# A decoder layer with PEER retrieval on one core: the residual of the last 256 tokens as DMA and VectorE work instead of products, and the first convolution rows fetched by ScalarE

## The chip, the core and the metric

The kernel runs on one core of a Trainium2 chip. The metric is the device time of one execution in microseconds (us). The engines are written as in the profile: PE (TensorE matmul; PEld is its weight load), DVE (VectorE), ACT (ScalarE), POOL (GpSimd), SP (SyncE). DMA transfers are issued by SP, ACT or POOL, each with a queue of its own (q1, q10 and q0 in the profile), and carried out by 16 DMA engines.

## The reference, cut to what matters

One layer, 512 prompt tokens and 32 sample tokens (8 sequences of 4), 1024 wide:

```python
proj = x @ w_in + b_in                     # q, k, v, g, ca, cg, 512 columns each
o, r_new = retention(rope(q), rope(k), v, r0)
ret_out = silu(g) * head_norm(o)
u = ca * sigmoid(cg)                       # depthwise convolution of width 31 over time
conv_out = silu(layer_norm(conv31(u) + dw_bias))
x1 = layer_norm(ALPHA * x + concat(ret_out, conv_out) @ w_out, ln1)
...
# PEER: 8 heads, the best 16 of 128 x 128 experts each
ffn = sum over the 128 chosen experts of gate * gelu(u[idx] . x1) * v[idx]
y = layer_norm(ALPHA * x1 + ffn, ln2)
```

The change touches two places of this: how `ALPHA * x1` gets into the last line for the last 256 prompt tokens, and how `u` gets into the convolution.

## The kernel before

The program is one function, `tile_step`, whose instructions a scheduler then orders on each engine by its own estimate of times; `behind(a, b)` fixes that `a` stands behind `b` where the author wants it, `await_` adds a wait. So an edit in one place can change the interleaving elsewhere.

**The first part** (up to about 400 us) is the projections, retention, convolution and output projection. A first pass handles 128 prompt tokens and the 32 samples, whose x1 is ready early; VectorE begins to retrieve experts for these (`gather0`) while the later tokens go through the mixer. The depthwise convolution of the later tokens (`later_conv`) runs on PE: for each of four channel groups m, `glu` makes u (line 290), `store_u` writes it to a DRAM tile `u_dram[m]` by a DMA of ACT (line 322), `tap_rows` fetches it back in four DMAs of SP, 206 KB each, each shifted by one column (line 330, tile `blk`), and `conv_taps` multiplies the rows by tap matrices (line 345, 64 records for one m). Nothing but the wait for the fetches separates `conv_taps` of m = 0 from the retention products (line 523) ahead of it. SP meanwhile issues weight loads (line 152) in program order.

**Then the mixer.** `mix_mm` computes the output projection and adds the residual as products: `residual` multiplies a 128-column block of x1 (or x), held transposed, by `scaled`, ALPHA on the diagonal (line 579). `mix_b` normalises (lines 560 to 574: `bn_stats`, `bn_aggr`, the subtraction, the reciprocal root, the scaling) and gives x1. For the first NG2 = 160 tokens (32 samples and 128 prompt tokens) it writes x1 to the DRAM tile `x1_dram` (line 967), from which it is loaded later. For the last 256 it keeps only the transposed copy `x1T`.

**Then the experts, in two ways at once.** The tokens up to NG2 and the first 128 are handled by *gathers*: POOL fetches a chosen expert's row of u and v (8 KB for each of 128 tokens, line 741), DVE takes the dot product (747), ACT the GELU and the gate (759, 764), DVE accumulates (769). The last 256 tokens, of which nearly all experts are computed densely, use PE: `scores_of` multiplies every expert's u with x1T (line 1039; SP loads u in 0.5 MB pieces at line 1037), `first_keys` and `last_keys` build the gates for each expert by products of one-hot matrices A and B (B by DVE, line 1156; products at 1175; the gates are then copied or multiplied into Ga to Gd at 1188 to 1191), and `v_products` accumulates gate times v over 128 groups of experts in four PSUM banks `pB` (line 1234; v loaded at 1229). The gathers beside it are released by `marks`, the products of the v stages, so that POOL doesn't run ahead.

Before the v stages start, `residual` fills the four banks `pB` with ALPHA * x1 by 16 calls, and all later products accumulate on top (`start=False`). The banks therefore hold the whole sum in the end, and the last norm reads them: `layer_norm(t, 128, ln[0], ln[1], pB[b], True)`, with the outputs stored by SP (line 1341). `phases` orders the last products so that b = 0 is complete first, then half 0 and half 1 of b = 1. `finish` is the same for the gathered tokens: it adds ALPHA * x1 to the accumulator by DVE (line 776) and normalises.

Of the kernel before, what the change touches and what calls it, by code (L numbers as in the profile page):

```python
# [8 lines left out]
F32 = mybir.dt.float32  # L9
# [7 lines left out]
OP = mybir.AluOpType  # L17
# [3 lines left out]
D = 1024  # L21
# [4 lines left out]
CW, CK = 512, 31  # L26
PH, NK, TK = 8, 128, 16
PAST = 4096
ALPHA = 2.0 ** 0.25
EPS = 1e-5  # L30
NR = NT - 128
NG2 = NS + 128
# [71 lines left out]
def tile_step(ctx: ExitStack, tc: tile.TileContext, a, o):  # L104
    nc = tc.nc
    V, S, T, G = nc.vector, nc.scalar, nc.tensor, nc.gpsimd

    per = ctx.enter_context(tc.tile_pool(name="per", bufs=1))
    gp = ctx.enter_context(tc.tile_pool(name="gp", bufs=3))
# [6 lines left out]
    dr = ctx.enter_context(tc.tile_pool(name="dr", bufs=1, space=bass.MemoryType.DRAM))  # L116
# [6 lines left out]
    banks = [ps0]  # L123
    turn = [0]

    steps, u_dram, updates, placed = {}, {}, [], []

    def mmps():
        turn[0] += 1
# [49 lines left out]
    ln = []  # L179

    def shared():
        return per.tile([128, 2 * D], F32, name="ln")
# [13 lines left out]
    def behind(ins, other):  # L196
        tc.add_manual_dep(ins.ins, other.ins.name, mybir.DependencyInfo(
            mybir.DependencyClass.NoSync, mybir.DependencyReason.DATA), reason="order")
# [29 lines left out]
    def rsqrt(dst, var):  # L228

        G.tensor_scalar(dst, var, EPS, None, op0=OP.add)  # L230
        G.tensor_tensor(dst, dst, mhalf[:dst.shape[0]].to_broadcast(list(dst.shape)), op=OP.pow)
# [4 lines left out]
    u_p = fe.tile([128, 4, CK + NP], F32, name="u_p")  # L236
# [82 lines left out]
    def store_u(m, L, p0):  # L319

        u_dram[m] = dr.tile([128, L + CK], F32, name=f"u_dram{m}")
        nc.scalar.dma_start(u_dram[m], u_p[:, m, p0:p0 + L + CK])

    def tap_rows(m, L, place):

        w = L + CK - 3
        rows = place[:, 0:4 * w].rearrange("p (g t) -> p g t", g=4)
        by_group = u_dram[m].rearrange("(g c) t -> c g t", g=4)
        for j in range(4):
            nc.sync.dma_start(rows[j * 32:j * 32 + 32], by_group[:, :, j:j + w])  # L330
        return rows

    def tap_weights(m):
# [219 lines left out]
    def layer_norm(t, n, g, b, src=None, table=False):  # L553


        st = gw.tile([128, 2, 6], F32, name="lst", bufs=3)
        mv = gw.tile([128, 2], F32, name="lmv", bufs=3)
        halves = [slice(q * 512, (q + 1) * 512) for q in range(2)]
        for q, c in enumerate(halves):
            V.bn_stats(st[:n, q], src[q][:n] if src else t[:n, c])  # L560
        V.bn_aggr(mv[:n], st[:n])
        rs = gw.tile([128, 1], F32, name="lrs", bufs=3)
        if table:
            S.activation(rs[:n], mv[:n, 1:2], AF.Sqrt, bias=eps_c[:n])
        else:
            rsqrt(rs[:n], mv[:n, 1:2])
        cs = halves if src else [slice(0, D)]
        for q, c in enumerate(cs):
            V.scalar_tensor_tensor(t[:n, c], src[q][:n] if src else t[:n, c], mv[:n, 0:1], g[:n, c],
                                   op0=OP.subtract, op1=OP.mult)  # L570
        if table:
            V.reciprocal(rs[:n], rs[:n])
        for c in cs:
            steps["ln"] = V.scalar_tensor_tensor(t[:n, c], t[:n, c], rs[:n], b[:n, c], op0=OP.mult, op1=OP.add)

    def residual(bank, xT, blocks, c0):

        for j, k in enumerate(blocks):
            T.matmul(bank[:, j * 128:(j + 1) * 128], xT[:, k, c0:c0 + 128], scaled, start=(j == 0), stop=False,
                     skip_group_check=True)  # L580
# [133 lines left out]
            return sb  # L714
        return score_of

    gx2, fence, held, marks, dots, listed = [], [], {}, [], [], []
    turns = ({}, {})

    def hold(k, ins):  # L720
# [3 lines left out]
    def gather(x1, idx, gate, acc, slots):  # L724

        late = len(slots) == 128 and x1 is not x1_0
        for k in slots:
            if x1 is x1_0:
                pools = (gp, gp, gp, gx, per) if k < K5 else (gp, gp, gp, gx) if k < KX else (gp, gp, gp, per)
                if KX <= k < K4[0] or k >= K4[1]:  # L730
                    pools = (gp,)
            elif late:
                pools = (gp, gp, gp, per if k < FREE else gx2[0]) if k < 60 else (gp, gp, gp, gx2[0], bx)
            else:
                pools = (gp, gp, gp, per) if k < len(slots) - 4 else (gp,)
            pool = pools[k % len(pools)]
            t = shared() if pool is per else pool.tile([128, 2 * D], F32, name="g")
            at = step(k) if late and k >= FREE else -1
            while at >= len(marks):
                yield  # L740
            fetch = G.indirect_dma_start(out=t, out_offset=None, in_=a["uv"],  # L741
                                         in_offset=bass.IndirectOffsetOnAxis(ap=idx[:, k:k + 1], axis=0))
            if at >= 0:
                tc.add_manual_dep(fetch.ins, marks[at].ins.name, mybir.DependencyInfo(
                    mybir.DependencyClass.Sync, mybir.DependencyReason.DATA), reason="pace")
            act = gw.tile([128, 2], F32, name="act")
            dot = V.scalar_tensor_tensor(t[:, :D], t[:, :D], 1.0, x1, op0=OP.mult, op1=OP.mult, accum_out=act[:, 0:1])  # L747
            if x1 is x1_0:
                for k0, ins in held.items():
                    if k >= k0:  # L750
                        behind(dot, ins)
            elif at >= 0:
                behind(dot, fence[0])
            turn = int((k - TURNS[0]) // TURNS[1]) + 1 if late and k >= TURNS[0] else -1
            if late and turns[1]:
                behind(dot, turns[1][min(max(turn, 0), len(turns[1]) - 1)])
            dots.append(dot)
            wgt = gw.tile([128, 1], F32, name="wgt")
            gate_ = S.activation(act[:, 1:2], act[:, 0:1], AF.Gelu)  # L759
            if x1 is x1_0 and k >= GATED and "scores" in steps:  # L760
                behind(gate_, steps["scores"])
            if turn > 0:
                behind(gate_, turns[0][min(turn, len(turns[0]) - 1)])
            S.activation(wgt, act[:, 1:2], AF.Copy, scale=gate[:, k:k + 1])  # L764
            v = t[:, D:]
            if k == slots[0]:
                S.activation(acc, v, AF.Copy, scale=wgt)
            else:
                V.scalar_tensor_tensor(acc, v, wgt, acc, op0=OP.mult, op1=OP.add)  # L769
            yield  # L770
# [18 lines left out]
                        break  # L789

    x1_0 = per.tile([128, D], F32, name="x1_0")
    x1_dram = dr.tile([NG2, D], F32, name="x1_dram")
    E0 = per.tile([128, PH, TK], F32, name="E0")
    GT0 = per.tile([128, PH, TK], F32, name="GT0")
    I0 = per.tile([128, PH * TK], I32, name="I0")
# [21 lines left out]
    both = lambda d0, d: [(0, 128, d0), (128, 160, d)]  # L817
# [12 lines left out]
    w = W0[2]  # L830
# [17 lines left out]
    for q in range(2):  # L848
        c = slice(q * 512, (q + 1) * 512)
# [13 lines left out]
    x1T, xT = xT, xT[:, :, NS:]  # L863
    banks[:] = [ps0]
    led = []
    for h0 in range(0, PH, 2):
        w = load_w(a["w_query"], h0 * 256)
        qq = small("qe", [128, 4, 128], bufs=1)
        for hs in ([h0], [h0 + 1]) if h0 == 0 else ([h0, h0 + 1],):
            for h in hs:  # L870
                for s in range(2):
                    m = (h - h0) * 2 + s
# [4 lines left out]
            c = V.tensor_copy(I0[:, ss], E0.rearrange("p h k -> p (h k)")[:, ss])  # L877
# [49 lines left out]
    for k, i in SLOTS_BEHIND:  # L927
        for dot in dots[k:]:
            behind(dot, updates[i])
    behind(placed[4], updates[1])  # L930
    banks[:] = [ps]
    rope(load_win(0), 0, xT, n - NS, 160, [(0, n - NS, qT)])
    later_keys = rope_steps(load_win(1), 1, xT, n - NS, 160, [(0, n - NS, kT)])
# [24 lines left out]
    xrs, pms, room = {}, {}, keys_or_scratch()  # L958
# [4 lines left out]

    def mix_b(c0, m, after=None):
        mix_norm(xrs[c0], m, x1T, c0, pms[c0], after)
        if c0 < NG2:
            nc.sync.dma_start(x1_dram[c0:min(c0 + m, NG2)], xrs[c0][:min(m, NG2 - c0)])

    norm_rows("ln1")
    gate_heads(ons[1], gT, NS)  # L970
# [80 lines left out]
    for h0 in range(0, PH, 2):  # L1051
        qs[h0 // 2] = (qs0, qs1)[h0 // 2 % 2]
        if h0:
            w = load_w(a["w_query"], h0 * 256)
# [4 lines left out]
        p0 = h0 % 4 * NS  # L1059
# [171 lines left out]

    def v_products(e, vt, b, qs=(0, 1)):
        W = place(e)
        return [T.matmul(pB[b][q], W[:, b * 128:(b + 1) * 128], vt[:, q * 512:(q + 1) * 512], start=False,  # L1234
                         stop=(e == NK - 1), skip_group_check=True) for q in qs]

    def v_stage(e):
# [44 lines left out]
    def step(k):  # L1282

        return k * 19 // 16
# [43 lines left out]
    pdn[0] = ctx.enter_context(tc.tile_pool(name="pdn", bufs=2, space=PSUM, reuse_waits="tile"))  # L1328
    pacc = ctx.enter_context(tc.tile_pool(name="pacc", bufs=1, space=PSUM, reuse_waits="tile"))
    pB = [[pacc.tile([128, 512], F32, name=f"pB{b}{q}") for q in range(2)] for b in range(2)]  # L1330
    for b in range(2):
        for q in range(2):
            residual(pB[b][q], x1T, range(q * 4, q * 4 + 4), NG2 + b * 128)
    gx2.append(ctx.enter_context(tc.tile_pool(name="gx2", bufs=1, reuse_waits="tile")))
    run((phases(), 1), (fetched(), 1))
    for b in range(2):
        t = gp.tile([128, 2 * D], F32, name="g")[:, :D]
        layer_norm(t, 128, ln[0], ln[1], pB[b], True)
        for q in range(2):
            c = slice(q * 512, (q + 1) * 512)  # L1340
            nc.sync.dma_start(o[0][0, 256 + b * 128:384 + b * 128, c], t[:, c])


# [44 lines left out]
```

## Time and profile before

| what | value |
|---|---|
| runs | 1436.52, 1442.21, 1444.98 us |
| median | 1442.21 us |
| the profiled execution's own time | 1439.42 us |
| its span in the trace | 1437.6 us |
| mean granted clock of PE | 0.993 |
| DMA | 511.01 MB, mean 355 GB/s |

The span runs from the first to the last recorded event; the remaining 1.8 us of the execution's time lie around it. All rows below are of that one execution. In a row of the timeline stand the start in us, the busy time in us, the engine, the line, the operation, what it writes and reads, how many instructions are drawn together, and in brackets the idle time of the engine just before and what ended it. "SPq" and "ACTq" are the issuing of DMAs. A row of the waits names the engine and line that waited, what released it, the sum in us, how often, and the longest. A row of windows has the window, its length, then busy time and instructions of PE, PEld, DVE, ACT and POOL, the granted clock of PE as a fraction of full speed, the busy share of the DMA engines and GB/s. A row of a DMA queue has packets, MB and their share of the engines' time.

Two pictures of the whole span help to place what follows. PE's busy tenths in 40 slices of 36 us stand in the first row, the clock in the second, the DMA engines' in the third:

```
PE   8999799999899999999999999999999999999998
PEclk9999899999999999999999999999999999999999
DMA  9859999988898799698699989999999999999995
```

### The profile page before, as it was taken

What the parts mean: (1) busy time and instruction counts of PE and PEld (TensorE: products, weight loads), DVE (VectorE), ACT (ScalarE), POOL (GpSimd) and SP (SyncE); (2) the same over time, 40 slices, a digit from 0 to 9 for tenths busy, and PEclk for the clock granted to TensorE, in tenths of its full rate; (3) what the DMA queues carried; (4) which work ended last, traced back from release to release, by engine and by line L of the source; (5) the groups of instructions that cost most, each with busy time, mean ns of one, the idle gap of its engine ahead of it and who ended that gap; (6) DMA issues with size and microseconds to landing.
All of it is one profiled execution on the core that took longest, in us unless ns stands there. A gap on an engine that the chain in (4) does not pass through costs nothing.

```text
span 1437.6 us, 19703 instructions
## 1 busy us (share of the span) xinstructions
PE 1395.3 (97%) x6766; PEld 960.1 (67%) x6766; DVE 1160.8 (81%) x2796; ACT 464.3 (32%) x1392; POOL 416.6 (29%) x407
## 2 busy tenths in 40 slices
PE   8999799999899999999999999999999999999998
PEld 8887365578667588887788884434445666666443
DVE  5949968988669999989999996987886966666666
ACT  1424422372122232244455541224653211111111
POOL 2172324334432222323123222233222222222220
PEclk9999899999999999999999999999999999999999
DMA  9859999988898799998699989999999999999995
GB/s 350 318 206 380 309 277 405 408 308 292 318 375 335 270 367 384 377 414 333 216 401 369 360 334 342 411 417 358 397 371 373 389 418 405 413 408 396 415 402 197
DMA packets 103281, 511.01 MB, mean 355 GB/s; under 512 B 10599, under 2 KB 24167, under 8 KB 60293
## 3 DMA queue, kind: packets, MB, share of 16 engines
q0 software_dynamic: 43392, 309.32, 55.2%
q1 hardware_dynamic: 54461, 193.48, 35.5%
q10 hardware_dynamic: 5328, 6.96, 1.4%
q8 instruction: 53, 0.87, 0.2%
q14 instruction: 47, 0.39, 0.1%
HBM read 503.49 MB, written 6.65 MB: 355 GB/s over the span
## 4 chain that ended last, share of the span: by engine, by line
PE 48%; DVE 26%; DMA 14%; issue 7%; ACT 3%; POOL 2%; SPq 0%; DVEq 0%; ACTq 0%; POOLq 0%
PE pB L1234 18%; PE sp L1039 17%; PE mm L255 8%; DVE acc L769 7%; DVE g L747 5%; DMA g<-in_uv_dram,Ib 4%; DMA g<-in_uv_dram,I 4%; DVE g L316 2%; PE mm L1175 2%; POOL g L741 1%; DMA ln<-in_uv_dram,I 1%; DMA cst<-in_consts_dram 1%; DMA blk<-u_dram 1%; PE mm L594 1%; DVE iu L640 1%
## 5 line engine op out<-in xcount | busy, mean ns | idle before, releaser
L1039 PE MATMUL sp<-x1T,uv 128*128 128x256 f32 x2048 | 460.5, 381 | 5.6 <-ACT Gb L1190 5.0
L1039 PEld LDWEIGHTS sp<-x1T,uv 128*128 128x128 f32 x2048 | 383.9, 190 | 71.8 <-issue 11.2
L769 DVE SCALAR_TENSOR_TENSOR acc<-g,wgt,acc 128x1024 f32<-128x1024 f32 x252 | 322.4, 1279 | 62.6 <-ACT wgt L764 60.7
L747 DVE SCALAR_TENSOR_TENSOR g<-g,x 128x1024 f32<-128x1024 f32 x255 | 309.9, 1217 | 64.7 <-DMA g<-in_uv_dram,Ib 34.2
L741 POOL DMA_INDIRECT g<-in_uv_dram,Ib x126 | 140.2, 1113 | 394.5 <-PE pB L1234 147.0
L759 ACT ACTIVATE act<-act 128x1 f32<-128x1 f32 x288 | 58.0, 202 | 565.1 <-DVE g L747 514.4
L741 POOL DMA_INDIRECT g<-in_uv_dram,I x104 | 136.6, 1314 | 302.2 <-DVE acc L769 177.7
L1234 PE MATMUL pB<-uv,Ga 128*128 128x512 f32 x352 | 158.9, 595 | 0.0
L255 PE MATMUL mm<-x1T,w 128*128 128x384 f32 (+1 forms) x448 | 152.7, 498 | 0.0
L255 PEld LDWEIGHTS mm<-x1T,w 128*128 128x128 f32 x448 | 84.5, 190 | 63.2 <-issue 31.2
L1234 PE MATMUL pB<-uv,Gb 128*128 128x512 f32 x256 | 111.6, 595 | 0.7 <-DMA uv<-in_uv_dram 0.5
L1234 PEld LDWEIGHTS pB<-uv,Ga 128*128 128x128 f32 x352 | 65.7, 190 | 66.6 <-issue 64.6
L1234 PE MATMUL pB<-uv,Gd 128*128 128x512 f32 x256 | 110.0, 592 | 0.0
L1234 PEld LDWEIGHTS pB<-uv,Gb 128*128 128x128 f32 x256 | 48.0, 190 | 63.5 <-issue 56.0
L1234 PEld LDWEIGHTS pB<-uv,Gd 128*128 128x128 f32 x256 | 48.6, 190 | 60.8 <-issue 59.3
L1234 PE MATMUL pB<-uv,Gc 128*128 128x512 f32 x160 | 72.2, 600 | 0.2
L1140 ACT ACTIVATE A<-row,e1T 128x128 f16<-128x128 bf16 x216 | 65.8, 391 | 5.9 <-PE mm L1175 5.8
L1188 ACT ACTIVATE W<-sp 128x256 f32<-128x256 f32 (+25 forms) x84 | 26.7, 318 | 120.2 <-PE sp L1039 118.7
L255 PE MATMUL mm<-g,w 128*128 128x160 f32 (+1 forms) x512 | 65.3, 287 | 0.0
L255 PEld LDWEIGHTS mm<-g,w 128*128 128x128 f32 x512 | 64.4, 191 | 0.6
L741 POOL DMA_INDIRECT g<-in_uv_dram,Is x25 | 33.6, 1344 | 77.5 <-DVE acc L769 38.7
L1191 DVE TENSOR_TENSOR Gd<-Gd,W 128x256 f32<-128x256 f32 x32 | 13.6, 424 | 48.4 <-ACT W L1188 48.4
(326 smaller groups left out, 1707.5 us busy)
## 6 DMA issues: line engine op xcount, KB each, us to landing
uv<-in_ut_dram SPq DMA_DIRECT2D x128, 512.0 KB
uv<-in_uv_dram SPq DMA_DIRECT2D x128, 512.0 KB
w<-in_w_in_dram SPq DMA_DIRECT2D x18, 1024.0 KB
w<-in_w_query_dram SPq DMA_DIRECT2D x15, 1024.0 KB
w<-in_w_out_dram SPq DMA_DIRECT2D x7, 1024.0 KB
blk<-u_dram SPq DMA_DIRECT2D x16, 206.0 KB
ln<-in_ln_g_dram POOLq DMA_DIRECT2D x5, 512.0 KB
ln<-in_ln_b_dram POOLq DMA_DIRECT2D x5, 512.0 KB
```

The lines of the kernel that those rows point to most:

```text
L255: T.matmul(p[:, :n], w[m // 2][:, k, (m % 2) * 128:(m % 2 + 1) * 128], xT[:, k, c0:c0 + n], start=(k == 0), stop=(k == 7))
L316: V.scalar_tensor_tensor(y[:, m], u_p[:, m, p0 + k:p0 + k + L], dw[:, m, k:k + 1], y[:, m], op0=OP.mult, op1=OP.add)
L594: last = T.matmul(banks_[q][:, s * 256:(s + 1) * 256], src[:, k, c0:c0 + C], wo[q * 2 + s][:, k0 + k, :], start=(xT is None and k0 == 4 an ...
L741: fetch = G.indirect_dma_start(out=t, out_offset=None, in_=a["uv"], in_offset=bass.IndirectOffsetOnAxis(ap=idx[:, k:k + 1], axis=0))
L747: dot = V.scalar_tensor_tensor(t[:, :D], t[:, :D], 1.0, x1, op0=OP.mult, op1=OP.mult, accum_out=act[:, 0:1])
L759: gate_ = S.activation(act[:, 1:2], act[:, 0:1], AF.Gelu)
L769: V.scalar_tensor_tensor(acc, v, wgt, acc, op0=OP.mult, op1=OP.add)
L1039: mm = T.matmul(sp[:, i], u[:, k], x1T[:, k, NG2:], start=(k == 0), stop=(k == 7), skip_group_check=True)
L1140: made = S.activation(A[:, t], row, AF.Abs, bias=e1T[:, t1 + t:t1 + t + 1])
L1175: mm = T.matmul(pt[:, t % nt], A[t % TB], B[:, q, t % TB // 2, :, t % 2], start=(q == 0), stop=(q == 1))
L1188: S.activation(W[:, :n], sp[:, :n], AF.Gelu)
L1234: return [T.matmul(pB[b][q], W[:, b * 128:(b + 1) * 128], vt[:, q * 512:(q + 1) * 512], start=False, stop=(e == NK - 1), skip_group_check= ...
```

## The change

Three edits that belong to two ideas. First, `mix_b` stores all of x1 to a larger `x1_dram` (two more DMAs of 512 KB on SP), the four residual calls ahead of the v stages go, the first v product of each bank starts the sum, and behind the v stages ACT fetches the x1 of each half of the 256 tokens (two DMAs of 512 KB) into the upper half of the tile in which the norm works; DVE adds ALPHA times it to the bank, 512 columns at a time (four `scalar_tensor_tensor`), and the norm then reads the tile in SBUF instead of the banks. Second, the four fetches of rows m = 0 are issued by ACT instead of SP; the store of u for m = 1 is put behind the last fetch issued so far, and the gates of the gathers from the seventh on are put behind the fourth fetch, both without a wait.

```diff
@@ store_u, tap_rows
-        nc.scalar.dma_start(u_dram[m], u_p[:, m, p0:p0 + L + CK])
+        store = nc.scalar.dma_start(u_dram[m], u_p[:, m, p0:p0 + L + CK])
+        if m == 1:
+            behind(store, fetched_[-1])
...
-            nc.sync.dma_start(rows[j * 32:j * 32 + 32], by_group[:, :, j:j + w])
+            load = (nc.sync if m else nc.scalar).dma_start(rows[j * 32:j * 32 + 32], by_group[:, :, j:j + w])
+            fetched_.append(load)
@@ gather
             gate_ = S.activation(act[:, 1:2], act[:, 0:1], AF.Gelu)
+            gates.append(gate_)
@@ behind later_conv
+    for gate_ in gates[6:]:
+        behind(gate_, fetched_[3])
@@
-    x1_dram = dr.tile([NG2, D], F32, name="x1_dram")
+    x1_dram = dr.tile([NG2 + 256, D], F32, name="x1_dram")
@@ mix_b
-        if c0 < NG2:
-            nc.sync.dma_start(x1_dram[c0:min(c0 + m, NG2)], xrs[c0][:min(m, NG2 - c0)])
+        nc.sync.dma_start(x1_dram[c0:c0 + m], xrs[c0][:m])
@@ v_products
-        return [T.matmul(pB[b][q], W[:, b * 128:(b + 1) * 128], vt[:, q * 512:(q + 1) * 512], start=False,
+        return [T.matmul(pB[b][q], W[:, b * 128:(b + 1) * 128], vt[:, q * 512:(q + 1) * 512], start=(e == 0),
@@ the end
-    for b in range(2):
-        for q in range(2):
-            residual(pB[b][q], x1T, range(q * 4, q * 4 + 4), NG2 + b * 128)
...
     for b in range(2):
-        t = gp.tile([128, 2 * D], F32, name="g")[:, :D]
-        layer_norm(t, 128, ln[0], ln[1], pB[b], True)
-        for q in range(2):
-            c = slice(q * 512, (q + 1) * 512)
+        both = gp.tile([128, 2 * D], F32, name="g")
+        t, x1 = both[:, :D], both[:, D:]
+        nc.scalar.dma_start(x1, x1_dram[NG2 + b * 128:NG2 + b * 128 + 128])
+        halves = [slice(q * 512, (q + 1) * 512) for q in range(2)]
+        for q, c in enumerate(halves):
+            V.scalar_tensor_tensor(t[:, c], x1[:, c], ALPHA, pB[b][q], op0=OP.mult, op1=OP.add)
+        layer_norm(t, 128, ln[0], ln[1], [t[:, c] for c in halves], True)
+        for q, c in enumerate(halves):
             nc.sync.dma_start(o[0][0, 256 + b * 128:384 + b * 128, c], t[:, c])
```

The scheduler's orders move with it; the rows below are instructions in the order of one engine, and from 322 on the line numbers of the changed kernel are 2 to 5 higher. On ACT, where the second and third u are stored (line 322; line 285 is the sigmoid of the gated unit, 759 and 764 the gate of a gather, 703 the exponential of a softmax), before:

```order
L703 ACT_TABLE_LOAD
L703 ACTIVATE ex<-ex 128x32
L322 DMA u_dram_1852<-u_p 128x415
L759 ACT_TABLE_LOAD
L759 ACTIVATE act<-act 128x1
L764 ACTIVATE wgt<-act,GT_135 128x1
L285 ACT_TABLE_LOAD
L285 ACTIVATE sg<-mm,cols 128x384
L322 DMA u_dram_1883<-u_p 128x415
```

And the same place on ACT in the changed kernel:

```order
L706 ACT_TABLE_LOAD
L706 ACTIVATE ex<-ex 128x32
L332 DMA blk<-u_dram_1815 32x4x412 x4
L322 DMA u_dram_1852<-u_p 128x415
L285 ACT_TABLE_LOAD
L285 ACTIVATE sg<-mm,cols 128x384
L762 ACT_TABLE_LOAD
L762 ACTIVATE act<-act 128x1
L768 ACTIVATE wgt<-act,GT_135 128x1
L322 DMA u_dram_1883<-u_p 128x415
```

The four fetches of m = 0 stand ahead of the store of m = 1, and one gate now follows the sigmoid where it came before it. On SP the four are gone from behind the weight loads.

On PE, the last scores ahead of the v stages (line 1039), the residual products and the first v products (line 1234) before:

```order
L1039 MATMUL sp<-x1T,uv 128x256 x16
L579 MATMUL pB_6864<-scaled,x1T 128x128 x4
L579 MATMUL pB_6865<-scaled,x1T 128x128 x4
L579 MATMUL pB_6866<-scaled,x1T 128x128 x4
L1039 MATMUL sp<-x1T,uv 128x256 x8
L579 MATMUL pB_6867<-scaled,x1T 128x128 x4
L1234 MATMUL pB_6864<-uv,Gb 128x512
L1234 MATMUL pB_6865<-uv,Gb 128x512
```

And in the changed kernel:

```order
L1180 LDWEIGHTS A
L1180 MATMUL mm<-B,A 128x96
L1044 MATMUL sp<-x1T,uv 128x256 x24
L1239 MATMUL pB_6866<-uv,Gb 128x512
L1239 MATMUL pB_6867<-uv,Gb 128x512
```

The 16 calls of line 579 are gone and the 24 scores around them stand together. Ahead of the first key groups on PE (line 1087 transposes the retrieved lists, line 214 is the warming of the clock with products of ones), before:

```order
L1087 MATMUL mm<-cst_89,eg 128x128 x2
L1039 MATMUL sp<-x1T,uv 128x256 x16
L1087 MATMUL mm<-cst_89,e_4246 128x128
L1087 MATMUL mm<-cst_89,eg 128x128 x2
L1039 MATMUL sp<-x1T,uv 128x256 x40
L214 LDWEIGHTS iot
```

And in the changed kernel:

```order
L1092 MATMUL mm<-cst_89,eg 128x128 x2
L1044 MATMUL sp<-x1T,uv 128x256 x16
L1092 MATMUL mm<-cst_89,e_4248 128x128
L1092 MATMUL mm<-cst_89,eg 128x128 x2
L1044 MATMUL sp<-x1T,uv 128x256 x32
L214 LDWEIGHTS iot
```

32 scores in place of 40 stand ahead of the warming; the other eight follow behind it, and from there to the v stages the scores and the key groups (line 1175) interleave in other portions. Elsewhere, on SP the two new stores of x1 stand between the fourth query weight load and the first four loads of u (line 1037). On ACT the two fetches of x1 stand between the last gate of the gathers and the square root's table load. On DVE the end reads: sum and statistics of half 0 of b = 0, the same of half 1, the norm of b = 0 with the sum of b = 1's half 0 ahead of its last two operations, then statistics of that half, the sum and the statistics of b = 1's half 1, and its norm.

More of the change, by code (lines that the diff above doesn't have):

```diff
@@ L124, in tile_step @@
     turn = [0]
-    steps, u_dram, updates, placed = {}, {}, [], []
+    steps, u_dram, updates, placed, fetched_ = {}, {}, [], [], []
     def mmps():
@@ L715, in fresh @@
         return score_of
-    gx2, fence, held, marks, dots, listed = [], [], {}, [], [], []
+    gx2, fence, held, marks, dots, gates, listed = [], [], {}, [], [], [], []
     turns = ({}, {})
```

## The prediction, made before the changed kernel ran

> **What bounds the kernel now.** I read the first part of the page, then the grouped waits of TensorE (PE), then the stages by windows.
>
> ```profile
> PE 1395.3 (97%) x6766; PEld 960.1 (67%) x6766; DVE 1160.8 (81%) x2796; ACT 464.3 (32%) x1392; POOL 416.6 (29%) x407
> PE 48%; DVE 26%; DMA 14%; issue 7%; ACT 3%; POOL 2%; SPq 0%; DVEq 0%; ACTq 0%; POOLq 0%
> PE mm L345 <- DMA blk<-u_dram: 6.3, 1, 6.3
> PE sp L1039 <- ACT Gb L1190: 5.0, 3, 2.7
> PE mm L620 <- DVE xr L574: 2.6, 1, 2.6
> PE mm L1175 <- DVE B L1156: 2.2, 7, 0.5
> 500.00:600.00 100.00, 99.80 (x474) 85.65 (x474) 99.94 (x335) 31.17 (x84) 27.79 (x23) 1.00 0.98 375
> 860.00:1040.00 180.00, 178.00 (x648) 80.12 (x647) 147.04 (x366) 61.63 (x173) 53.45 (x45) 1.00 0.97 382
> ```
>
> PE is busy for 1395.3 of 1437.6 us, so it is the bound by the mean: 42.3 us of idleness in all, the longest single wait being the 6.3 us of the convolution's first products (L345) for their rows. But the chain of waits gives PE only 48%. In 500 to 600 PE works 99.80 us of 100 and VectorE (DVE) 99.94; in 860 to 1040 PE works 178.00 of 180 while the DMA engines are busy 0.97 of the time. So a microsecond taken from PE counts only if DVE and the gathers don't hold it back a little later. That is the question for both halves of this change.
>
> **First rows, fetched by ACT.**
>
> ```profile
> 149.10 0.33 SPq L152 DMA_DIRECT2D w<-in_w_in_dram  x1
> 149.48 3.35 SPq L330 DMA_DIRECT2D blk<-u_dram  x4
> 150.77 0.23 ACT L703 ACTIVATE ex<-ex 128x32 f32<-128x32 f32 x1
> 155.08 0.34 ACTq L322 DMA_DIRECT2D u_dram<-u_p  x1
> 165.36 1.55 PE L523 MATMUL mm<-on,ktok 32*128 32x256 f32 x4 [1.60 <-DVE states L525]
> 173.26 8.02 PE L345 MATMUL mm<-blk,taps 128*32 128x384 f32 x64 [6.35 <-DMA blk<-u_dram]
> 230.70 5.37 PE L345 MATMUL mm<-blk,taps 128*32 128x384 f32 x64
> 150.00:155.00 5.00, 5.00 (x17) 2.91 (x16) 5.00 (x22) 0.98 (x2) 1.99 (x3) 1.00 1.01 326
> 165.00:170.00 5.00, 1.55 (x4) 0.83 (x4) 5.00 (x12) 2.38 (x9) 0.26 (x1) 0.50 1.01 366
> 177.00:179.00 2.00, 2.00 (x20) 0.82 (x16) 0.76 (x2) 0.00 (x0) 1.47 (x1) 0.58 1.03 415
> q1 hardware_dynamic: 190, 1.06, 81.3%
> q0 software_dynamic: 70, 0.57, 84.8%
> q1 hardware_dynamic: 71, 0.13, 20.8%
> 191.91 0.62 DVE L290 SCALAR_TENSOR_TENSOR u_p<-mm,cols,sg 128x384 f32<-128x384 f32 x1 [6.57 <-PE mm L255]
> ```
>
> Before, SP (SyncE) issues a 1 MB weight load at 149.10 and right behind it the four fetches of m = 0, 206 KB each. They land so late that PE, done at 166.91 (165.36 + 1.55), starts L345 at 173.26. Its granted clock is 0.50 meanwhile and until about 178.7 (a window of 2 us with 0.58), so the 64 products take 8.02 us where the same 64 take 5.37 at 230.70. So 6.35 of waiting and 2.65 of slow clock, 9.0 us, are the most that the fetches could return.
>
> How much of it? The last two queue rows are those of 156 to 158: the gathers' queue q0 sent 70 packets and SP's q1 71. They go one for one, 70 in 2 us, on 16 engines 0.45 us per pair. Each fetch is 128 runs, all four 512, or 32 per engine: 32 x 0.45 = 14.4 us, whichever queue holds them, as long as the gathers go on. What the new place saves is the time behind the weight load. The first queue row is of 150 to 154: SP's queue moved 1.06 MB, the weight load and hardly a row. At the 326 GB/s of 150 to 155 the load alone takes 3.2 us, so the rows began between 152.3 (149.10 + 3.2) and 154. After, ACT issues the four behind ex (150.77 + 0.23 = 151.0; as SP needs 3.35 for four, each takes 0.8 or so, the last at about 154), and the first can move at 151. The lead is 1.3 to 3 us; I take 2.0: L345 at about 171.3. The slow clock may end earlier by as much, or by more; I take 1.0 out of the 2.65. Together **-3.0**, with 0 and -9.0 as ends. Nothing queues up behind the new issues: the next ACT instruction of before was the store at 155.08, after an idle stretch for DVE. That store and those of m = 2 and 3 now stand behind the rows on ACT's queue; rows m = 1 wait for the first of them, but are needed only by the second L345 group, 18 us later.
>
> Does it last? DVE's row at 191.91 waits 6.57 us for PE, so DVE starts that stretch when PE does, and the gain passes to both engines.
>
> The Trainium skill's page "DMA: Bandwidth & Descriptors" (section "Issuing engines are not separate DMA queues") speaks against this half: DMAs started by different engines run on the same 16 DMA engines and interleave, and a second issuing engine saves only the sequencer's issue time. By that rule the term is 0 in place of -3.0. The one-for-one packets agree with the interleaving; that the weight load is served ahead on the same queue isn't covered by it.
>
> **Residual products removed.**
>
> ```profile
> 851.65 2.84 PE L579 MATMUL pB<-scaled,x1T 128*128 128x128 f32 x24
> 854.33 3.62 PE L1039 MATMUL sp<-x1T,uv 128*128 128x256 f32 x16
> 857.78 1.05 PE L579 MATMUL pB<-scaled,x1T 128*128 128x128 f32 x8
> 858.67 21.62 PE L1234 MATMUL pB<-uv,Gb 128*128 128x512 f32 x50
> 872.25 7.35 DMA x<-x_dram
> 885.53 12.74 DMA g<-in_uv_dram,Ib
> 1014.45 0.73 PE L1175 MATMUL mm<-B,A 128*128 128x32 f16 x16 [0.48 <-DVE B L1156]
> 1034.57 0.64 PE L1175 MATMUL mm<-B,ss 128*128 128x32 f16 x16 [0.36 <-DVE B L1156]
> 1035.40 0.73 PE L1175 MATMUL mm<-B,A 128*128 128x32 f16 x16 [0.20 <-DVE B L1156]
> ```
>
> The 16 calls are 32 records. They occupy PE from 851.65 to 854.33 and from 857.78 to 858.67: 2.68 + 0.89 = 3.57 us, with no idleness beside them. So the products of group b (L1234) start 3.57 us sooner. But at 1014.45, 1034.57 and 1035.40 PE waits for DVE's B: it comes there just in time already. DVE's work up to there runs through the load of x1 (7.35) and gathers (12.74), in pieces of the chain in time order, at a DMA share of 0.97, and the residual products aren't in that chain. What PE gains at 858 is waited off there as far as DVE isn't earlier too. DVE can be earlier a little, since the gathers of this stage are released by marks on PE's products. Ends -3.57 and 0; I take **-1.5**, nearer to the waits.
>
> **The tail.**
>
> ```profile
> 1422.83 0.70 DVE L560 BATCH_NORM_STATS2 lst<-pB 128x6 f32<-128x512 f32 x1 [3.54 <-PE pB L1234]
> 1413.37 1.29 DVE L776 SCALAR_TENSOR_TENSOR g<-x,acc 128x512 f32<-128x512 f32 x2
> 1414.58 1.28 DVE L560 BATCH_NORM_STATS2 lst<-g 128x6 f32<-128x512 f32 x2
> 1424.77 5.74 PE L1234 MATMUL pB<-uv,Gd 128*128 128x512 f32 x13
> 1430.55 0.70 DVE L560 BATCH_NORM_STATS2 lst<-pB 128x6 f32<-128x512 f32 x1 [2.35 <-PE pB L1234]
> 1431.53 1.41 DVE L569 SCALAR_TENSOR_TENSOR g<-pB,lmv,ln 128x512 f32<-128x512 f32 x2
> ```
>
> PE ends at 1430.51; from there everything is in line. One half of the sum is added by DVE after that: one more operation, at 0.65 (half of L776) to 0.70 (half of L569's 1.41, which reads PSUM, as this does). What follows reads SBUF: statistics 0.64 in place of 0.70, L569 1.28 in place of 1.41. Sum 0.70 - 0.06 - 0.13 = **+0.5** (0.4 to 1.4, the latter if the half before is late as well). The three other additions lie in the waits of 3.54 and 2.35 us. The two fetches of x1 stand on ACT behind the last wgt (about 1412); with the 7.35 us of the like load they are there by 1420, before 1422.83.
>
> **Stores of x1.**
>
> ```profile
> 373.00 27.53 SPq L1037 DMA_DIRECT2D uv<-in_ut_dram  x4
> 391.03 1.41 DVE L574 SCALAR_TENSOR_TENSOR states<-states,lrs,ln 128x512 f32<-128x512 f32 x2 [0.46 <-POOL lrs L231]
> 428.62 0.60 PE L1039 MATMUL sp<-x1T,uv 128*128 128x256 f32 x2
> ```
>
> On SP the two stores stand ahead of the first four ut loads, and the second waits until DVE has written its x1 (392.44). The loads begin there instead of at 373.00, but are first used at 428.62; the last of the four was issued about 400 anyway. 36 us cover a 0.5 MB load. I put it at 0; if that cover is gone, the same 1 MB as the weight load, 3 us. The added 2 MB are 0.4% of 511.
>
> **Order.** The scheduler also interleaves PE, ACT and DVE anew from about 430 to 860: 32 products L1039 rather than 40 stand ahead of the 24 warming ones, and groups of L1175 are cut elsewhere. No work is added; I put it at 0, within 3 either way (half of the 7.2 below).
>
> **Sum.** -3.0 - 1.5 + 0.5 + 0 = -4.0 on the profiled execution's 1439.42 gives 1435.4. That execution lies 2.8 us below the median shown (1442.21) and inside the runs' 1436.52 to 1444.98; I forecast 1436 us.
>
> **Rivals.**
>
> *Both gains in full*: the rows land in time (-9.0), DVE's B comes as much earlier as PE does (-3.57), tail +0.5: 1427.4. For it: PE is 97% busy and the wait stands alone. Against it: 32 rounds of 0.45 us, at a start of 152, end at 166.4 only if nothing else interleaves, and the store of m = 1 and the weight load's rest do. With one gain full and the other half, 1431.
>
> *Nothing arrives*: the rows are as late as before, since ACT issues 1.5 us later than SP did (151.0 against 149.48) and shares the same engines, and the 3.57 us end in the wait at 1014 to 1036; +0.5 from the tail: 1439.9. This is also the case in which the fetches don't do what they should. For it: one packet each per round; against it: the weight load's 3 us go.
>
> *Slower*: PE runs short at the first key groups. There it waits already for ACT's Gb (5.0) and DVE's B (7 waits, 2.2), both set by DVE, which is full in 500 to 600. With 8 products L1039 fewer ahead (8 x 3.62 / 16 = 1.8 us), PE arrives 1.8 us earlier and waits as much longer; if the newly cut groups double the waits too, 7.2 + 1.8 + 0.5 = +9.5, 1448.9 without any gain. It decides only from DVE not coming earlier by as much as PE; it becomes slower than before once the added waits pass 4.5 us. Against it: the products moved are still to be done later and fill other waits.
>
> **How the numbers follow.** Forecast (1431 to 1440) 0.50, both gains in full or nearly 0.24, nothing 0.14, slower 0.12. 0.5% is 7.2 us, about what a measurement of this kernel can tell from no change: the forecast's 4 lies within it. Faster by over 0.5%: the full case and some of the forecast, 0.32; slower 0.10; within, 0.58. The range takes in the full case at its low end, 1427, and reaches toward the slower one to 1446.
>
> **What would show it.** In the changed profile: L345's first group at 171.3 rather than 173.3, its 64 products at 7.0; a start before 168 would prove the full case, 173 or later the empty one. L1234 follows the last L1039 at once; the sum of waits of L1175 on B at 1010 to 1036 grows from 1.0 to about 3 if the gain is eaten there. From PE's last product to the end 0.5 us more than before. If PE's waits on Gb and B pass 12 us in 640 to 860, the slower case holds. If DVE in 300 to 500 waits more for gathers than before, then the gain at 173 was lost to DMA.

## The result, and the profile after

| | before | changed |
|---|---|---|
| median of 7 runs each | 1439.81 us | 1449.09 us |
| lowest and highest | 1436.36, 1444.98 | 1448.12, 1454.18 |
| profiled execution's span | 1437.6 us | 1446.3 us |

The ratio is 1.0058, 95% interval 1.0034 to 1.0082: the change costs 0.58%, about 8 us. In a second series of 13 runs beside 29 of before it was 1.0052 (1.0033 to 1.0071). That is slower than the range that was forecast, and on the other side of no change.

The grouped waits of PE, changed kernel (engine, line and what it makes, what released it: sum in us, times, longest):

```profile
PE mm L348 <- DMA blk<-u_dram: 6.2, 1, 6.2
PE mm L1180 <- DVE B L1161: 5.4, 8, 3.3
PE sp L1044 <- ACT Gb L1195: 4.3, 5, 1.3
PE mm L655 <- DMA keys<-in_keysT_dram: 4.0, 1, 4.0
```

The first row is the wait that the new fetches were to shorten: 6.3 before, 6.2 now. The last row is new. Before, no product waited for `keys<-in_keysT_dram`, a 1 MB load of the sub-keys that ACT issues for the key scores of the expert lists (L655, 652 before). The prediction didn't name it. What became of it, in the timelines of SP, ACT and PE of the changed kernel:

```profile
371.19 0.33 SPq L972 DMA_DIRECT2D x_dram<-keys  x1
388.21 0.33 SPq L972 DMA_DIRECT2D x_dram<-states  x1
388.85 8.65 SPq L1042 DMA_DIRECT2D uv<-in_ut_dram  x4
382.07 0.29 ACT L768 ACTIVATE wgt<-act,GT 128x1 f32<-128x1 f32 x1
389.36 0.20 ACT L762 ACTIVATE act<-act 128x1 f32<-128x1 f32 x1 [7.00 <-DVE g L750]
389.60 0.29 ACT L768 ACTIVATE wgt<-act,GT 128x1 f32<-128x1 f32 x1
389.81 0.35 ACTq L636 DMA_DIRECT2D keys<-in_keysT_dram  x1
402.26 1.62 PE L655 MATMUL mm<-keys,qs 128*128 128x128 f32 x6 [4.00 <-DMA keys<-in_keysT_dram]
405.81 1.80 PE L655 MATMUL mm<-keys,qs 128*128 128x128 f32 x10 [1.92 <-ACT qs L1007]
407.54 24.51 PE L255 MATMUL mm<-x1T,w 128*128 128x416 f32 x64
```

And the same place before:

```profile
374.62 0.36 ACTq L633 DMA_DIRECT2D keys<-in_keysT_dram  x1
401.93 0.83 PE L652 MATMUL mm<-keys,qs 128*128 128x128 f32 x6
404.75 1.05 PE L652 MATMUL mm<-keys,qs 128*128 128x128 f32 x10 [1.98 <-ACT qs L1002]
405.73 22.61 PE L255 MATMUL mm<-x1T,w 128*128 128x416 f32 x64
```

The key load goes into a tile that lies over the one from which the first added store reads (`x_dram<-keys`). So it now also has to wait for that store, and the scheduler put it two gates of gathers further back in ACT's queue: 59 gates stand ahead of it, not 57. The first of these waits 8.45 us for DVE, and DVE 8.27 of them for the gather (its dot product starts at 380.57); the second waits 7.00 us for DVE, which normalises the last x1 in between (384.91 to 388.19). The load is issued at 389.81 instead of 374.62, 1 us behind the first of the four loads of u, which itself waited on SP for the second store (the other three follow at 395 to 397). It arrives in a stretch in which the DMA engines are full. The DMA queues of the changed kernel from 394 to 400 (packets, MB, share of the 16 engines):

```profile
q10 hardware_dynamic: 123, 1.00, 39.8%
q0 software_dynamic: 132, 1.00, 39.4%
q1 hardware_dynamic: 146, 0.52, 21.4%
```

and before, in the same 6 us:

```profile
q0 software_dynamic: 306, 2.17, 98.1%
```

Before, the gathers had these 6 us alone and got 2.17 MB; now the keys (q10) and the loads of u (q1) take 61% and the gathers get 1.00 MB. So PE waits 4.00 us for the keys, and DVE 11.20 us for a gather where it waited 5.88 (changed, then before):

```profile
402.41 1.23 DVE L750 SCALAR_TENSOR_TENSOR ln<-ln,x 128x1024 f32<-128x1024 f32 x1 [11.20 <-DMA ln<-in_uv_dram,I]
```

```profile
401.35 1.23 DVE L747 SCALAR_TENSOR_TENSOR ln<-ln,x 128x1024 f32<-128x1024 f32 x1 [5.88 <-DMA ln<-in_uv_dram,I]
```

Part of the longer wait is that DVE came earlier. Counted from the first product on the samples' x1 (369.98 and 372.02, from PE's timelines), this row starts 3.1 us later than before.

The idle stretch has a second price. Windows of the changed kernel (PE, PEld, DVE, ACT, POOL busy, PE's granted clock, DMA share, GB/s), then of before:

```profile
400.00:407.00 7.00, 2.82 (x14) 2.28 (x16) 4.59 (x7) 1.90 (x7) 0.00 (x0) 0.58 1.03 424
407.00:415.00 8.00, 8.00 (x22) 4.22 (x19) 5.77 (x7) 1.30 (x5) 5.64 (x4) 0.72 0.88 327
403.00:411.00 8.00, 6.08 (x20) 3.52 (x19) 7.78 (x12) 3.19 (x12) 2.93 (x2) 0.50 0.92 348
```

```profile
400.00:407.00 7.00, 5.02 (x39) 4.03 (x39) 5.66 (x8) 3.22 (x11) 0.66 (x1) 1.00 1.01 415
```

The clock falls to half (0.50 from 403 to 411), and the 64 weight products behind it take 24.51 us instead of 22.61. To compare runs, whose start differs, I measure one stage: from the first product on the samples' x1 (`mm<-cst,xr`, 372.02 before) to the first score (`sp`, 428.62 before). It took 56.6 us before and 62.4 in the changed kernel (369.98 to 432.34).

### The profile page after: what moved, and what is told of

The parts are those of the page before. It is cut to its first block, busy times and chain, and to the rows that moved or that the text cites. A ratio compares the mean times of both kernels' runs of the same rounds, so it can differ in the third digit from the quotient of the medians.

```text
span 1446.3 us, 19656 instructions
## 1 busy us (share of the span) xinstructions
PE 1399.4 (97%) x6734; PEld 959.8 (66%) x6734; DVE 1163.0 (80%) x2800; ACT 460.8 (32%) x1391; POOL 428.5 (30%) x407
## 4 chain that ended last, share of the span: by engine, by line
PE 32%; DVE 17%; DMA 13%; issue 4%; ACT 1%; POOL 0%; DVEq 0%; POOLq 0%
PE pB L1239 19%; PE sp L1044 12%; DVE acc L773 5%; DMA g<-in_uv_dram,Ib 3%; DVE g L750 3%; DMA uv<-in_ut_dram 3%; DMA g<-in_uv_dram,I 3%; DMA g<-in_uv_dram,Is 2%; DMA uv<-in_uv_dram 1%; PE mm L1180 1%; DVE B L1161 1%; DVE ln L750 1%; DMA ln<-in_uv_dram,I 1%; DVE iu L646 1%; DVE iu L643 1%
## 5 line engine op out<-in xcount | busy, mean ns | idle before, releaser
L744 POOL DMA_INDIRECT g<-in_uv_dram,Ib x126 | 144.5, 1147 | 392.8 <-PE pB L1239 129.9
L744 POOL DMA_INDIRECT g<-in_uv_dram,I x104 | 143.9, 1383 | 295.9 <-DVE acc L773 158.4
L1239 PEld LDWEIGHTS pB<-uv,Gb 128*128 128x128 f32 x256 | 48.2, 190 | 62.2 <-issue 54.9
L744 POOL DMA_INDIRECT ln<-in_uv_dram,I x24 | 33.5, 1398 | 70.9 <-DVE acc L773 57.3
```

## The experiments

Theory K (keys): the loss is the late load of the keys. Rivals: G, the key groups that the scheduler cut anew (640 to 860); E, the end of the kernel (DMA at its limit from 1230 on, a longer tail). All ratios are to the runs of before on the same chip, with their 95% interval. A microsecond of loss is worked out as the ratio times 1444, the median of before in these series.

**The stores alone.** In the kernel before:

```diff
-    x1_dram = dr.tile([NG2, D], F32, name="x1_dram")
+    x1_dram = dr.tile([NG2 + 256, D], F32, name="x1_dram")
-        if c0 < NG2:
-            nc.sync.dma_start(x1_dram[c0:min(c0 + m, NG2)], xrs[c0][:min(m, NG2 - c0)])
+        nc.sync.dma_start(x1_dram[c0:c0 + m], xrs[c0][:m])
```

> The kernel before, with the two added stores of x1 and nothing else of the change (the residual stays in products, SP fetches the rows; what is stored isn't read). Theory K (keys): the stores put the 1 MB load of the keys behind two more gates on ACT, to about 392 in place of 374.6, where it collides with the loads of u that SP issues behind the second store; the first key products then wait for it and run at half clock. K expects 5 to 10 us more than before, the wait of the key products on the load at 3 to 7 us, and the first scores at about 434 in place of 428.6. Rival G (key groups): the loss comes from the newly cut first key groups around 658 in the changed kernel; then the stores alone cost under 2 us. Rival E (end): the loss comes from DMA at its limit in 1230 to 1310 and the longer tail; under 2 us here too.

Measured: 1.0043 (1.0020 to 1.0066), 6 us slower. Key load issued at 390.4, a wait of 4.45 us for it, 24.25 us for the 64 products, the stage 62.7 us:

```profile
403.28 1.62 PE L652 MATMUL mm<-keys,qs 128*128 128x128 f32 x6 [4.45 <-DMA keys<-in_keysT_dram]
408.55 24.25 PE L255 MATMUL mm<-x1T,w 128*128 128x416 f32 x64
```

So most of the loss comes with two stores that nothing reads, and not from the end of the kernel (E), which is as before here. Contrary to what was expected, this run doesn't separate G: the stores alone bring the new cut of the key groups as well. From the warming products to the first v product PE's order in the trace (residual products aside) is that of the changed kernel, record by record. The runs below with the keys early have this cut too, and they decide.

**Each half of the change alone.** First the half with the sum on DVE (the changed kernel with SP fetching the rows, and without the two orders on ACT):

```diff
...
-            load = (nc.sync if m else nc.scalar).dma_start(rows[j * 32:j * 32 + 32], by_group[:, :, j:j + w])
+            load = nc.sync.dma_start(rows[j * 32:j * 32 + 32], by_group[:, :, j:j + w])
...
-    for gate_ in gates[6:]:
-        behind(gate_, fetched_[3])
```

> The first half of the change alone: stores, no residual products, the sum on DVE at the end; SP fetches the rows as before. K expects the stores' 5 to 10 less up to 3.6 for the products plus 1 for the tail: 3 to 8 us slower than before. G: also slower if its first key groups are cut as in the changed kernel. If the stores are harmless, 3 to 0 us faster.

Measured: 1.0030 (1.0011 to 1.0049), 4 us slower, with a wait of 4.24 us for the keys and a stage of 62.8 us. Then the other half, the kernel before with the rows fetched by ACT:

```diff
...
-            nc.sync.dma_start(rows[j * 32:j * 32 + 32], by_group[:, :, j:j + w])
+            load = (nc.sync if m else nc.scalar).dma_start(rows[j * 32:j * 32 + 32], by_group[:, :, j:j + w])
+            fetched_.append(load)
...
+    for gate_ in gates[6:]:
+        behind(gate_, fetched_[3])
```

> The second half of the change alone: ACT fetches the first rows; residual products and stores as before. The load of the keys stays where it was on ACT. K expects 1 to 3 us faster than before: the first rows' products start about 1 us earlier and end about 2 us earlier. G or E: the same or slower, if the later stages don't pass the gain on.

Measured: 1.0015 (0.9991 to 1.0039), no difference that can be told, and no gain. PE waited 6.49 us for the rows. The keys were on time (issued at 377.7, no wait for them). The stage still took 58.6 us and the 64 products 24.31, behind a wait of 2.57 us for ACT's copy of the queries: the slow clock comes without late keys as well.

**The keys moved ahead.** In the changed kernel:

```diff
+        load = steps["keys"] = q.dma_start(keys[0], a["keysT"])
...
             gates.append(gate_)
+            if x1 is x1_0 and k >= 57:
+                behind(gate_, steps["keys"])
```

> The changed kernel with one order added: the gates of the gathers from number 58 on stand behind the load of the keys on ACT. K expects the load issued at about 377 (when the store of the tile under it has landed) and landed before 390, no wait of the key products on it, and 5 to 8 us less than the changed kernel: 1441 to 1444. G and E expect the changed kernel's time, within 2 us.

Measured: 1.0015 (0.9994 to 1.0036) against the changed kernel's 1.0052 and 1.0058: some 5 to 6 us back by one order (the intervals just overlap). ACT's and PE's timelines of this run, at the place shown above:

```profile
381.39 0.35 ACTq L636 DMA_DIRECT2D keys<-in_keysT_dram  x1
401.88 0.49 PE L655 MATMUL mm<-keys,qs 128*128 128x128 f32 x2 [1.61 <-ACT qs L1009]
404.82 22.61 PE L255 MATMUL mm<-x1T,w 128*128 128x416 f32 x64
```

No wait on the keys, full clock, and the stage at 55.4 us. The load went at 381.39 and not at 377: ACT had nothing else to do from 375.5 on, and SP had issued the store of the tile under it at 373.53, 7.9 us earlier. So the load does wait for the store, and this alone costs nothing in the stage. SP's loads of u still stood behind the second store here (from 390.67), so in this stage their delay alone costs nothing.

**The changed kernel again**, beside the next runs:

> The changed kernel itself once more, beside the runs below on one chip. It should again be 5 to 12 us slower than before, with a wait of about 4 us of the key products on the load of the keys and their weight products at half clock (24 to 25 us for 64).

Measured: 1.0052 (1.0033 to 1.0071). Its profiled execution was the fastest of the 13, at a span of 1438.0, and still had a wait of 3.67 us for the keys, 24.27 us for the 64 products and a stage of 62.2 us. One execution's span says less than a stage does: between the two profiles of this same program lie 8 us, of which 3 to 4 fall between 640 and 860 and as much again where DMA is at its limit behind 1230.

**The late keys alone.** The kernel before with only the load's place changed:

```diff
+        load = steps["keys"] = q.dma_start(keys[0], a["keysT"])
...
+            if x1 is x1_0 and k == 58:
+                behind(steps["keys"], gate_)
```

> The kernel before with one order added and nothing of the change: the load of the keys on ACT stands behind gate number 59 of the gathers, as in the changed kernel. Theory K (the late key load is the cause) expects 3 to 7 us more than before: the load issued at about 392, a wait for it or at least half a clock at the key products. If 1 to 2 us or nothing, then the load is harmless where SP's loads of u don't collide with it, and the collision behind the store counts.

Measured: 1.0011 (0.9987 to 1.0036), too little to tell. The load went at 387.08 with the loads of u already out (from 369.16). The stage was 60.5 us:

```profile
399.93 0.49 PE L652 MATMUL mm<-keys,qs 128*128 128x128 f32 x2 [4.06 <-ACT qs L1004]
404.38 23.99 PE L255 MATMUL mm<-x1T,w 128*128 128x416 f32 x64
```

PE waited for ACT's copy of the queries, which stood behind a gate whose gather was late; the keys' last packet had run by 397. So the stage is 3.9 us longer than before, by another way; with the loads of u behind the store it is 6. That the late load delayed this gather isn't shown. Over the runs with SP's or ACT's rows behind the weight load, the stage was 55.4 with u late and keys early, 60.5 with keys late and u early, 62.2 to 62.8 with both late (four profiles), and 55.9 to 58.6 with neither late (five, the three below with the keys ahead among them).

**Keys ahead, and the last store behind them on ACT**, in the changed kernel (the order of the run above, and):

```diff
-        nc.sync.dma_start(x1_dram[c0:c0 + m], xrs[c0][:m])
+        steps["kept"] = (nc.sync if c0 < known else nc.scalar).dma_start(x1_dram[c0:c0 + m], xrs[c0][:m])
...
     load_keys(pool=rk)
+    behind(steps["kept"], steps["keys"])
```

> The changed kernel with the load of the keys ahead of gate number 58, and the store of the last 128 rows of x1 issued by ACT behind it, so that SP's first loads of u don't wait for it. K expects no wait on the keys and the loads of u issued from about 371; the time 5 to 9 us below the changed kernel, within 3 of before. If the rest of the loss lies in the newly cut key groups at 640 to 860 (theory G), it stays 2 to 4 us above before.

Measured: 1.0021 (1.0005 to 1.0038), below the changed kernel, but 3 us above before. The stage is 55.9 us.

**The stores with both orders, without the rest**: the first experiment with the two orders of the last.

> The kernel before with the two added stores of x1 (not read), the load of the keys ahead of gate number 58, and the last store issued by ACT behind it. Theory K (the stores cost because they push the key load into the loads of u) expects what the stores alone cost, 0.43%, to go: within 2 us of before, and from the samples' x1 products (mm<-cst,xr) to the first scores 55 to 57 us, as before (56.6) and not 62.7. If the stores cost by themselves (1 MB more, DVE's x1 held longer), 4 to 6 us above before.

Measured: 0.9999 (0.9979 to 1.0018). Of the stores' 0.43% nothing is left that can be told. The stage is 57.2 us. The key groups are cut as in the changed kernel here too, so their cut isn't what the 0.43% came from.

**The same with the sum on DVE**, so that the way of adding the residual is the only difference from the last run:

> The same with the residual products removed and the sum on DVE at the end, the rows fetched by SP: the first half of the change without the late keys. From the stage itself: 3.6 us of products gone, 1.0 more in the tail, about 2 waited off on DVE's B at 1000 to 1040: 0 to 2 us below the run with the stores alone and the keys ahead. If all 3.6 count, 2.5 below; if the products are waited off entirely, 1 above.

Measured: 1.0009 (0.9994 to 1.0024): within 2 us of the last run and of before. The removed products bring nothing that the total shows. Against the same half with the keys late (1.0030) it is 3 us less, and the two intervals overlap; the stage is 58.2 us in place of 62.8.

**Rows ahead of the weights.** Two versions of the kernel before. In the first the loads of one weight block go behind the rows on SP (three loads moved), in the second only the load at 149.10:

```diff
-        w = load_win(2)
+        w = load_w(a["w_in"], 1024, after=steps["rows"][3])
```

```diff
-    rope(load_win(0), 0, xT, n - NS, 160, [(0, n - NS, qT)])
+    rope(load_w(a["w_in"], 0, after=steps["rows"][3]), 0, xT, n - NS, 160, [(0, n - NS, qT)])
```

> The kernel before with SP's weight loads of the block for v ordered behind the first rows' fetches, so that nothing stands ahead of the rows on SP's queue. If the 1 MB ahead held the rows back, their first packets leave within 1 us of the issue at about 149, and the first products start near 168 to 170. If each such fetch takes about 3.8 us from its issue to its first packet wherever it is issued, the packets begin at about 153 as before and the products start at 171 to 173. The weights come later, so the total may be longer.

> The kernel before with the first rows' fetches ahead of the one weight load on SP's queue (it follows them); nothing else. If a large load ahead holds back whatever queue follows it, the rows' first packets leave at about 150.5 in place of 153, and the first tap products start at 168 to 170 in place of 171 to 173: 2 to 5 us faster than before where the gain lasts. If the rows are held by the gathers' packets alone, no change.

Measured: the first 1449.44 us in its one run, the second 0.9994 (0.9978 to 1.0010). In both PE no longer waits for the first rows (in the first version it then waits 3.74 us for the second). In the second the products start right behind the retention products; but look at what is late next, in its PE timeline:

```profile
168.31 7.42 PE L345 MATMUL mm<-blk,taps 128*32 128x384 f32 x64
232.87 7.57 PE L345 MATMUL mm<-blk,taps 128*32 128x384 f32 x64 [4.84 <-DVE g L747]
```

There the last group's products (230.70 before, with no wait) wait 4.84 us for DVE's work beside the gathers, and run 7.57 us in place of 5.37. The samples' x1 then comes at 380.16, against 372.02. The 5 us of lead are gone, and the total is that of before.

**All three mended**: the sum on DVE, the keys ahead with the store behind, and the rows ahead of one load.

> All three mended: the sum on DVE, the keys ahead and the last store behind them, and the rows ahead of the weight load on SP. If the parts add up, faster than before by 2 to 6 us and faster than the changed kernel by 9 to 14. If DVE and the gathers set the middle stage (450 to 620), the early gains are given back there and it comes out within 2 us of before.

Measured: 1.0020 (0.9998 to 1.0042). The first rows' products start at 166.53, and the last group's at 231.08 with no wait: the lead is lost here as well, but before that place. No version beat the kernel before.

## Why the prediction was wrong, step by step

**The step that failed is the stores of x1**, put at 0. It followed the loads of u that wait on SP, found 36 us of cover for them, and that part held (stage 55.4 us with u late and keys early). It did not ask who else uses the tiles that the stores read. The key load does: it was on ACT's queue, its tile lies over one of them, and the new dependence moved it two gates back, into a full stretch of DMA. Price some 6 us: measured with the stores alone, and gone when two orders undo it, 1.0043 to 0.9999. The other pairs give 5 to 6 us (the changed kernel and the run with one order), 5 (with both orders) and 3 (the half with the sum on DVE), each to within about 4. So K is shown as the main cause. How the stage's 6 us reach the end isn't: the run with ACT's fetches alone and the second rows-first run come to the first score at 433.3 and 432.1, as late as the four with late keys (431.2 to 433.7), with no loss in the total that can be told. The fallback price of 3 us given there for a lost cover was for the wrong load.

**First rows, -3.0 taken, 0 measured.** The rows' wait was 6.35, 5.09, 4.16, 5.11, 4.29 and 3.40 us in the six profiles with SP's fetches behind the weight load, 4.7 on the mean, and 6.16, 6.49, 4.29, 3.03 and 5.83 in the five with ACT's, 5.2. On SP's queue the weight load ahead held the rows, as the working said: with the rows ahead of it the wait goes. What was wrong is that a queue of its own escapes it. The changed kernel's ACT timeline, then its DMA queues from 151 to 154 and from 154 to 156:

```profile
150.52 3.03 ACTq L332 DMA_DIRECT2D blk<-u_dram  x4
```

```profile
q1 hardware_dynamic: 106, 0.78, 70.2%
q0 software_dynamic: 23, 0.14, 21.8%
...
q0 software_dynamic: 70, 0.57, 73.6%
q1 hardware_dynamic: 19, 0.12, 15.1%
q10 hardware_dynamic: 46, 0.08, 10.2%
```

Issued at 150.52, the fetches have no packet until 154, when the weight load on q1 is nearly through; then they run one for one with the gathers, as forecast. By the packets of the traces, the rows' first one runs 5.4 to 5.9 us behind the issue of the weight load in the five profiles with ACT's fetches, and 3.9 to 4.0 in the six with SP's: ACT's rows begin later, not earlier.

The Trainium skill says in "DMA: Bandwidth & Descriptors" (section "Issuing engines are not separate DMA queues") that a second issuing engine saves only the time of issuing. The trace agrees in that nothing was gained: by that rule the term was 0. I had given the rival that carries it 0.14.

**And a gain there would not have lasted.** "DVE starts that stretch when PE does, and the gain passes to both engines" isn't borne out: with the wait removed, the lead is gone by 232.87, behind a wait of 4.84 us for DVE, and the total is unchanged (0.9994).

**Residual products: the size was close, the mechanism shown in part.** From the first v product to the first on Gd the seven profiles with the residual products take 460.5 us on the mean (459.4 to 461.8), the seven without 462.5 (460.1 to 464.3). So of the 3.57 us about 2.1 are given back behind 858, and some 1.5 stay, as forecast; the ranges overlap, so these means are good to little better than 1 us. Of the 2.1, 1.1 us lie between the first v product and the first on Ga, the stretch that holds the waits on B (192.2 against 191.1 us on the mean), and 1.0 between Ga and Gd (270.4 against 269.4). PE's waits on B from 1000 to 1045 us sum to 1.1 us on the mean without the products (0 to 2.4) and 0.7 with them (0 to 1.5), so B shows as a taker of some 0.4 only, and single profiles scatter by more than that. In the changed kernel they sum to 0.95, and not to the 3 that was named as the sign. That time is given back there agrees with the forecast; that B is what takes it was not shown, so the close size is in part luck.

**The tail: +0.5 taken, +1.0 measured.** From PE's end to the end of the span it is 7.0 to 7.2 us in the seven profiles with the residual products and 8.05 to 8.11 in the seven without. DVE of the changed kernel:

```profile
1438.23 0.69 DVE L1344 SCALAR_TENSOR_TENSOR g<-g,pB 128x512 f32<-128x512 f32 x1 [0.71 <-PE pB L1239]
1438.95 0.69 DVE L563 BATCH_NORM_STATS2 lst<-g 128x6 f32<-128x512 f32 x1
1439.92 1.41 DVE L572 SCALAR_TENSOR_TENSOR g<-g,lmv,ln 128x512 f32<-128x512 f32 x2
```

The addition is 0.69, as taken. The savings weren't there: the statistics take 0.69 and the subtraction 1.41 out of SBUF, as out of PSUM. The 1.28 that I quoted was two statistics drawn as one row, or one operation of 1024 columns, and not two of 512 that stand apart. Together with the products, 1.5 - 1.0 leaves a gain of 0.5 us, which 0.9999 and 1.0009 neither show nor contradict.

**Order: 0 within 3.** It held as a term. From the first score to the first v product, three profiles with the old cut take 430.0 to 431.7 us, and three with the new cut and the residual products 433.6 to 435.1, 3 us more. From there to the end these three are shorter, 576.6 to 577.2 us against 577.8 to 579.0. In the total nothing of it shows: two of the three with the new cut are the runs with 0.9999 and 0.9994. So G, as the cause of the loss, is out.

The rival "slower" named 1448.9 us, and 1449.09 was measured. That is luck: its sign, waits of PE on Gb and B above 12 us in 640 to 860, isn't there (8.8 us in the changed kernel, 6.2 before), and the loss lies elsewhere. Its working also took 8 products of the order for 1.8 us; they are 16 records of the trace, 3.6 us.

With the keys early the changed kernel is still 2 to 3 us above before (1.0015 and 1.0021, the latter clear of 0 by its interval). Where this part comes from stays open; ACT's fetches alone (-1 to +6 us) don't settle it.

## What to carry to other kernels

A store that nothing waits for is still a reader of its tile: list whatever is loaded into that memory next, on every queue, and look up in the order where that load then stands and behind which waits. Moving the rows to another issuing engine didn't make them start earlier behind a large load that had been issued just before; ordering them ahead of it did. And where PE, DVE and the gathers are all nearly full, compare one stage across runs before crediting a saving: here 5 us gained at 168 were gone by 233, and of 3.6 at 858 about 2 were given back by 1320. The stage itself depends on when it starts: in the three rows-first runs it starts 4 to 8 us later than before and takes only 52 to 53 us.

## What the runs showed of the hardware that I had not expected

The time from the rows' issue to their first packet varied with what had been issued just before. In the second rows-first run SP issued the rows at 150.53, ahead of the weight load, and from 151 to 153 it had already sent 86 packets:

```profile
q0 software_dynamic: 66, 0.48, 71.5%
q1 hardware_dynamic: 86, 0.13, 27.8%
```

By the packets of the traces it took 1.3 to 1.4 us in the three runs with the rows ahead, 3.5 to 3.6 in the six behind the weight load on SP, and 3.7 to 4.2 in the five from ACT. That the weight load makes the whole of ACT's delay isn't shown: in the run with the late keys alone, ACT's key load took 2.7 us to its first packet, with no packet of SP's queue in the 3 us before its issue or in between. And the same program's executions differed by more than many of the parts studied here: 1439.75 to 1455.58 us in 13 runs of the changed kernel.
